# A two-layer decoder trunk on one core: the conditioning product moves from VectorE to four column groups of TensorE, the first projections run by pairs of row blocks, and the convolution's projections become three products of float32r parts

## The chip, the cores and the metric

One Trainium2 chip, one of its cores. The metric is the device time of one execution in microseconds (us), and less is better.

## The reference

256 tokens of width 1024 go through two layers. A vector `c` sets, through `silu(c)` and one large matrix per layer, six vectors of 1024 numbers per layer (shift, scale and gate of the mixer, and of the experts).

```python
cond = silu(c)                                        # 1 x 1024
for layer in range(2):
    mod = cond @ ada_w[layer] + ada_b[layer]          # 1 x 6144
    sh1, sc1, g1, sh2, sc2, g2 = split(mod, 6)
    h = rms_norm(x, norm_mix[layer]) * (1 + sc1) + sh1
    y = nsa_conv_mixer(h) if layer == 0 else rwkv_pool_mixer(h)
    x = x + g1 * y
    h = rms_norm(x, norm_ffn[layer]) * (1 + sc2) + sh2
    x = x + g2 * grouped_moe(h)                       # 16 experts of width 512, 2 per token
return rms_norm(x, final_norm)
```

In layer 0 `h @ w_in` gives queries, keys and values of a sparse attention (compressed blocks, selected blocks, window) and three blocks of 512 columns `xb, bg, cg` of a short convolution, `y = bg * conv3(cg * xb)`. In layer 1 it gives the inputs of an RWKV-7 scan and of a pooling. All data are float32.

## The kernel before, in words

The whole trunk is one program. It has four stages, one after the other: mixer 0 (attention and convolution), the experts of layer 0, mixer 1 (RWKV and pooling), the experts of layer 1. All weights are streamed: SyncE (SP) issues them as tiles of 128 x 2048 float32 (1 MB) into a ring of `NB = 10` buffers named `w`, which grows by some slabs of the mixers when these are free. A load into a ring buffer waits until the buffer's last reader is done, and all loads behind it on SP's queue wait with it.

The order on TensorE (PE) and on SP is written out by hand, as the order in which the Python code emits it. Chains that wait are filled by `Fill`: a list of small units of PE work, each with a cost in us, of which `fill.run(us)` emits as many as make up `us` at the point where it stands. The order on VectorE (DVE), ScalarE (ACT) and GpSimd (POOL) is chosen by a scheduler from a model.

**Conditioning** (`ada`, L203 to L213). `ada_w` is laid out transposed: a tile holds, for 128 output columns on the partitions, the 1024 input weights of two column blocks. `cond` is the vector `silu(c)` on every partition. For each half tile DVE does one pass over 128 x 1024 that multiplies by `cond` and sums along the row (L209), which leaves one column of `modc`; POOL adds the bias (L213). There are 12 groups (`n`) in each layer, of 2 tiles and 4 passes, so 48 MB and 96 passes in all. Layer 0 has all its groups in mixer 0, where layer 1's groups 0 to 2 are done too; group 3 (2 MB) comes between the experts of layer 0 and mixer 1, in `start` (L1618), and the others lie in mixer 1.

**First projections of mixer 0** (L477 to L480, L526 and on). For each half `h` of the rows of the weight: 8 passes of L209 (two groups), 8 transposes of the normed `xn` (L289), the modulation into `hT` (L278 on DVE, L280 on ACT), then the three projections `TokProj` (k and v, q, and the 280 other columns) with four row blocks each.

**Convolution's projections** (`chan_units`, L556). Three groups of 512 columns (xb, cg and bg), each four units of 8 float32 products 128x128 by 128x256 (L566), 96 products in all. They are fill for the waits of the attention.

**Attention**. The hidden part of the compression is `L605` (32-column stationary tiles, so four column groups of the array side by side), the gelu chain ends in `hg` (L625), then L634 and L639 make the compressed keys and values, L653 scores them, `L658` to `L667` are their softmax, L673 transposes it. Ten steps of a pipeline follow: scores L684 and L686, softmax L687 to L699, transposes L709 (evacuated by `evac`, L140 on DVE and L142 on ACT), output L720 and L724, with fill between.

**Experts**. L994 makes gate and up (64-column stationary tiles, two column groups), L1026 down, for 16 experts; the weights of one layer are 96 tiles of 1 MB, a third each for gate, up and down.

**Mixer 1**. Its weights are split into two float32r parts: `split_w` (L396 and L397) casts the high part on ACT and subtracts for the low part on DVE or POOL; `product` (L435) adds hi·hi, hi·lo and lo·hi. The RWKV chunk products L1331, a solve (L1349 and L1354) and its spread follow, then levels (L1383, L1374) and the scan.

Of the kernel before, what the change touches and what calls it, by code (L numbers as in the profile page):

```python
# [22 lines left out]
S = 256  # L23
# [4 lines left out]
NB = 10  # L28
# [68 lines left out]
def trunk(ctx: ExitStack, tc: tile.TileContext, A, out):  # L97
# [49 lines left out]
    nc.scalar.dma_start(cond, bass.AP(tensor=ca.tensor, offset=ca.offset, ap=[[0, 128], [1, D]]))  # L147
    P.activation(cond, cond, AF.Silu)  # L148
    x = act.tile([128, 2, D], F32, name="x")
    for tt in range(2):  # L150
        nc.scalar.dma_start(x[:, tt], A["x"][tt * 128:(tt + 1) * 128, :])
    vec = con.tile([128, NV], F32, name="vec")
# [7 lines left out]
    load_consts(con, "c_all", nc.scalar)  # L160

# [38 lines left out]
    def ada_load(l, n):  # L200
        return [stream(A["ada_w"][l, n, h]) for h in range(2)]

    def ada(l, n, tiles=None, h0=0, cs=(0, 1)):  # L203

        for h, w in enumerate(tiles or ada_load(l, n), h0):
            for c in cs:
                ws = w[:, c * D:(c + 1) * D]
                k = n * 4 + h * 2 + c
                V.scalar_tensor_tensor(ws, ws, 1.0, cond, op0=OP.mult, op1=OP.mult, accum_out=modc[:, l, k:k + 1])  # L209
        if h == 0 or c == 0:  # L210
            return
        o = V_ADAB + l * 48 + n * 4
        G.tensor_tensor(modc[:, l, n * 4:n * 4 + 4], modc[:, l, n * 4:n * 4 + 4], vec[:, o:o + 4], op=OP.add)  # L213

    def ada_pieces(l, n):

        tiles = ada_load(l, n)

        def piece(h, c, after):
            with tc.issue_after(after):  # L220
                ada(l, n, [tiles[h]], h, (c,))

        return [lambda after, h=h, c=c: piece(h, c, after) for h in range(2) for c in range(2)]
# [25 lines left out]
    class Norm:  # L249
# [32 lines left out]
        def scale(self, tt, r):  # L282
            V.tensor_scalar(self.xn[:, tt], x[:, tt], r, None, op0=OP.mult)

# [98 lines left out]
    class WGroup:  # L383


        def __init__(self, src, n):
            self.n = n
            self.h = [stream(src[:, h * 4 * n:(h + 1) * 4 * n], 4 * n) for h in range(2)]

        def __call__(self, kt, lo=0, hi=None):  # L390
            hi = self.n if hi is None else hi
            return self.h[kt // 4][:, (kt % 4) * self.n + lo:(kt % 4) * self.n + hi]
# [45 lines left out]
    def mixer0(after):  # L438
# [23 lines left out]
        class TokProj:  # L462
# [10 lines left out]
            def run(self, h):  # L473
                n = self.n
                for tt in range(2):
                    if h == 0:
                        self.pq[tt] = ps(n)  # L477
                    for k in range(4):
                        kt = h * 4 + k
                        mm(self.pq[tt], hT[:, kt, tt * 128:(tt + 1) * 128], self.w[:, k * n:(k + 1) * n], start=kt == 0, stop=kt == 7)  # L480
                    if h:
# [36 lines left out]
        projs = [TokProj(512, 512, done_k4), TokProj(0, 512, done_q), TokProj(1024, 280, done_k2)]  # L518
        for h in range(2):
            ada(0, h)  # L520
            ada(0, 2 + h)
            norm.ab(h)
            for tt in range(2):
                norm.transposes(tt, h)
            for t in projs:
                t.load(h)  # L526
                if h == 0 and t is projs[0]:
                    load_consts(mp, "c_m0", nc.sync)
                    G.tensor_copy(cbf, K("causal"))
                t.run(h)  # L530
# [3 lines left out]
        for n in (4, 5):  # L534
            ada(0, n)
# [20 lines left out]
        def chan_units(col, done):  # L556
            w = WGroup(W0[:, col * 8:(col + 512) * 8], 512)
            out = []
            for ct in range(4):
                st = {}  # L560

                def unit(q, ct=ct, st=st):
                    if q == 0:
                        st["pq"] = ps(S)
                    for kt in range(q * 4, q * 4 + 4):
                        mm(st["pq"], w(kt, ct * 128, ct * 128 + 128), hT[:, kt, :], start=kt == 0, stop=kt == 7)  # L566
# [3 lines left out]
                out += [(1.73, lambda q=q, u=unit: u(q)) for q in range(2)]  # L570
# [1130 lines left out]
```

## Time and profile before

| what | value |
| --- | --- |
| median of 3 runs | 841.82 us (840.27 to 2588.47) |
| the profiled execution | 841.15 us |
| span of its records | 839.4 us (1.75 us lie around it) |
| mean granted TensorE clock | 0.965 |
| HBM read | 289.4 MB |

The profiled execution is 0.67 us below the median. A row of a timeline reads: start, duration, engine, line and operation, what is written and read, shapes, how many records, and in brackets the idle time of the engine just before with what ended it. A row of groups reads: busy time, mean of one in ns, idle time before them and what ended it. A float32 matmul leaves two records, so "x24" of float32 are 12 products; a product of float32r parts leaves one. The stages are mixer 0 from 0 to 207 us, the experts of layer 0 to 414, mixer 1 to 621, the experts of layer 1 and the end to 839.4.

### The profile page before, as it was taken

What the parts mean: (1) busy time and instruction counts of PE and PEld (TensorE: products, weight loads), DVE (VectorE), ACT (ScalarE), POOL (GpSimd) and SP (SyncE); (2) the same over time, 40 slices, a digit from 0 to 9 for tenths busy, and PEclk for the clock granted to TensorE, in tenths of its full rate; (3) what the DMA queues carried; (4) which work ended last, traced back from release to release, by engine and by line L of the source; (5) the groups of instructions that cost most, each with busy time, mean ns of one, the idle gap of its engine ahead of it and who ended that gap; (6) DMA issues with size and microseconds to landing.
All of it is one profiled execution on the core that took longest, in us unless ns stands there. A gap on an engine that the chain in (4) does not pass through costs nothing. (4 is left out here: it accounts for less than half of the span.)

```text
span 839.4 us, 12129 instructions
## 1 busy us (share of the span) xinstructions
PE 752.2 (90%) x4833; PEld 423.1 (50%) x4834; DVE 440.7 (53%) x937; ACT 222.2 (26%) x442; POOL 101.6 (12%) x87
## 2 busy tenths in 40 slices
PE   0998989897999999999679869999979999999994
PEld 0556766455353353533278859567543534435341
DVE  5566869854122343322788898984531421434225
ACT  3031213244120121111457533303541201202112
POOL 0000132411000000000233793000110000000000
PEclk9999989998999999999879979999989999999998
DMA  9999859797999999999846185885849999999991
GB/s 363 415 421 420 355 195 364 287 419 282 374 422 423 421 422 421 423 420 424 330 189 251 63 324 216 337 317 200 346 177 421 422 422 422 422 422 422 420 417 74
DMA packets 42689, 291.34 MB, mean 347 GB/s; under 512 B 4864, under 2 KB 5504, under 8 KB 8448
## 3 DMA queue, kind: packets, MB, share of 16 engines
q1 hardware_dynamic: 41760, 288.07, 84.6%
q10 hardware_dynamic: 864, 2.40, 0.7%
q8 instruction: 42, 0.69, 0.3%
q14 instruction: 23, 0.19, 0.1%
HBM read 289.40 MB, written 1.05 MB: 346 GB/s over the span
## 5 line engine op out<-in xcount | busy, mean ns | idle before, releaser
L994 PE MATMUL ps<-w,XT 128*64 128x512 f32 x1024 | 223.7, 594 | 0.0
L994 PEld LDWEIGHTS ps<-w,XT 128*64 128x64 f32 x1024 | 75.4, 137 | 144.5 <-issue 140.3
L209 DVE SCALAR_TENSOR_TENSOR w<-w,cond 128x1024 f32<-128x1024 f32 x96 | 118.4, 1263 | 11.4 <-ACT cond L148 6.3
L999 DVE TENSOR_TENSOR sg<-sg,ps 128x512 f32<-128x512 f32 x16 | 11.0, 688 | 199.4 <-PE ps L994 199.4
L1026 PE MATMUL ps<-w,HT 128*64 128x512 f32 x512 | 113.8, 596 | 1.3 <-ACT HT L1013 1.3
L1026 PEld LDWEIGHTS ps<-w,HT 128*64 128x64 f32 x512 | 35.2, 137 | 70.5 <-issue 63.0
L435 PE MATMUL ps<-hT,wr 128*128 128x256 f32 x288 | 56.0, 297 | 5.6 <-issue 4.1
L370 PE MATMUL ps<-w,slab 128*128 128x512 f32 x128 | 59.7, 604 | 0.0
L1031 DVE SCALAR_TENSOR_TENSOR Y<-ps,gw,Y 128x512 fp32r<-128x512 f32 x32 | 24.0, 751 | 62.8 <-ACT Y L1030 62.8
L397 POOL TENSOR_TENSOR wr<-w,wr 128x2048 fp32r<-128x2048 f32 x5 | 24.7, 4945 | 224.1 <-SPq L1088 211.6
L435 PEld LDWEIGHTS ps<-hT,wr 128*128 128x128 f32 x288 | 47.6, 203 | 6.6 <-issue 4.6
L1030 ACT ACTIVATE Y<-ps,gw 128x512 fp32r<-128x512 f32 x32 | 21.9, 686 | 98.2 <-PE ps L1026 98.2
L381 DVE TENSOR_TENSOR x<-x,ps 128x512 f32<-128x512 f32 x72 | 46.3, 681 | 0.3
L566 PE MATMUL ps<-hT,w 128*128 128x256 f32 x192 | 46.1, 397 | 0.0
L380 DVE TENSOR_TENSOR ps<-ps,gb 128x512 f32<-128x512 f32 x64 | 41.4, 693 | 2.6 <-PE ps L1046 2.4
L435 PE MATMUL ps<-lo,wr 128*128 128x256 f32 x144 | 42.3, 294 | 0.0
L1046 PE MATMUL ps<-Y,CT 128*128 128x512 f32 x128 | 39.0, 421 | 2.9 <-ACT Y L1030 1.7
L566 PEld LDWEIGHTS ps<-hT,w 128*128 128x128 f32 x192 | 37.3, 199 | 6.1 <-issue 0.8
L480 PE MATMUL ps<-w,hT 128*128 128x512 f32 (+1 forms) x96 | 36.8, 544 | 0.3 <-ACT hT L280 0.2
L998 ACT ACTIVATE sg<-ps 128x512 f32<-128x512 f32 x16 | 9.6, 597 | 98.6 <-PE ps L994 98.6
L280 ACT ACTIVATE XT<-ps,AB 128x256 f32<-128x256 f32 x32 | 18.0, 563 | 62.2 <-PE ps L909 50.8
L370 PEld LDWEIGHTS ps<-w,slab 128*128 128x128 f32 x128 | 22.8, 190 | 22.4 <-issue 21.3
(321 smaller groups left out, 959.9 us busy)
## 6 DMA issues: line engine op xcount, KB each, us to landing
w<-in_moe_g_dram SPq DMA_DIRECT2D x64, 1024.0 KB, 16.0
w<-in_moe_u_dram SPq DMA_DIRECT2D x64, 1024.0 KB, 15.0
w<-in_moe_d_dram SPq DMA_DIRECT2D x60, 1024.0 KB, 16.1
w<-in_ada_w_dram SPq DMA_DIRECT2D x48, 1024.0 KB, 9.4
w<-in_w_dram SPq DMA_DIRECT2D x19, 1024.0 KB, 11.6
w<-in_wout_dram SPq DMA_DIRECT2D x8, 1024.0 KB, 9.7
w<-in_cmp_w_dram SPq DMA_DIRECT2D x4, 1024.0 KB, 12.6
w<-in_moe_d_dram SPq DMA_DIRECT2D x4, 512.0 KB, 17.9
```

Of the source, the lines that this page charges most:

```text
L209: V.scalar_tensor_tensor(ws, ws, 1.0, cond, op0=OP.mult, op1=OP.mult, accum_out=modc[:, l, k:k + 1])
L370: mm(st[h], self.oT(kt)[:, tt * 128:(tt + 1) * 128], self.ws[h][kt // 4][:, (kt % 4) * 512:(kt % 4 + 1) * 512], start=kt == 4, stop=kt == 3)
L380: V.tensor_mul(po, po, gb[:, sl])
L381: V.tensor_add(x[:, tt, sl], x[:, tt, sl], po)
L397: eng.tensor_tensor(lo, raw, hi, op=OP.subtract)
L435: mm(pq, a, b, start=first and kt == kts[0] and i == 0, stop=last and kt == kts[-1] and i == 2)
L480: mm(self.pq[tt], hT[:, kt, tt * 128:(tt + 1) * 128], self.w[:, k * n:(k + 1) * n], start=kt == 0, stop=kt == 7)
L566: mm(st["pq"], w(kt, ct * 128, ct * 128 + 128), hT[:, kt, :], start=kt == 0, stop=kt == 7)
L994: mm(pg[64 * e:64 * e + 64, :], XT[:, kt, 64 * e:64 * e + 64], ws[kt // 4, e][:, (kt % 4) * 512:(kt % 4 + 1) * 512], start=kt == 0, stop=k ...
L1026: mm(py[64 * e:64 * e + 64, :], HT[:, c, 64 * e:64 * e + 64], ws[e][:, c * 512:(c + 1) * 512], start=c == 0, stop=c == 3)
L1031: V.scalar_tensor_tensor(Y[:, 1, sl], py, gw, Y[:, 0, sl], op0=OP.mult, op1=OP.subtract)
L1046: mm(po, CT[:, tt], Y[:, i, h * 512:(h + 1) * 512], start=i == 0, stop=i == 1)
```

## The change

1. Of the conditioning only layer 0's groups 0 to 3 (16 passes, `cols`) stay on DVE. The other 40 tiles (same bytes, another layout, `ada_q`) are multiplied on PE by units of four matmuls, one for each column group, with a column of `silu(c)` spread to 32 columns as the stationary tile (L234 of the changed kernel). Eight units add up to one bank; ACT copies it (L238), four small matmuls (L243) turn it into columns, and DVE adds the bias (L246). The units are fill: 24 in mixer 0, 16 in mixer 1. Layer 1's group 3 is done in mixer 0 with the others of its 16 columns, so `start` has no conditioning left.
2. At the start `c` comes through two queues, and all loads of ACT's queue are issued before its first activation. The first projections run by pairs of row blocks: 4 passes, 4 transposes and two modulations, then k/v and q of that pair; the 280 other columns once per half.
3. The convolution's weights and `hT` are split into float32r parts, and each of the 96 products becomes three. The parts take ring buffers, two for each raw tile.
4. The ring has 11 buffers, and the gate's transposes, the load of the output projection and the pace of the fill have moved.

```diff
-NB = 10
+NB = 11
...
-    nc.scalar.dma_start(cond, bass.AP(tensor=ca.tensor, offset=ca.offset, ap=[[0, 128], [1, D]]))
-    P.activation(cond, cond, AF.Silu)
+    for eng, o in ((nc.sync, 0), (nc.scalar, 64)):
+        eng.dma_start(cond[o:o + 64], bass.AP(tensor=ca.tensor, offset=ca.offset, ap=[[0, 64], [1, D]]))
...
     load_consts(con, "c_all", nc.scalar)
+    P.activation(cond, cond, AF.Silu)
+    P.activation(ccol, ccol, AF.Silu)
...
-    def ada(l, n, tiles=None, h0=0, cs=(0, 1)):
-        for h, w in enumerate(tiles or ada_load(l, n), h0):
-            for c in cs:
-                ws = w[:, c * D:(c + 1) * D]
-                k = n * 4 + h * 2 + c
-                V.scalar_tensor_tensor(ws, ws, 1.0, cond, op0=OP.mult, op1=OP.mult, accum_out=modc[:, l, k:k + 1])
...
+        def unit(self, l, g, kt, w):
+            if kt == 0:
+                self.bank = ps(512)
+            for q in range(4):
+                mm(self.bank[32 * q:32 * q + 32, :], ccol[:, kt:kt + 1].to_broadcast([128, 32]), w[:, q * 512:(q + 1) * 512],
+                   start=kt == 0, stop=kt == 7)
+            if kt == 7:
+                self.row = con.tile([128, 512], F32, name="arow", tag="arow")
+                P.copy(self.row, self.bank)
+
+        def columns(self, l, g):
+            pc = ps(4, 4)
+            for c in range(4):
+                mm(pc[:, c], self.row[:, c * 128:(c + 1) * 128], ident[:, ::32], start=True, stop=True)
+            o = V_ADAB + l * 48 + g * 16
+            f = lambda t: t.rearrange("p (q c) -> p c q", q=4)
+            V.tensor_tensor(f(modc[:, l, g * 16:g * 16 + 16]), pc, f(vec[:, o:o + 16]), op=OP.add)
...
+        nxt = norm.pair(0)
         for h in range(2):
-            ada(0, h)
-            ada(0, 2 + h)
...
+            for q in (2 * h, 2 * h + 1):
+                for n in (h, 2 + h):
+                    cols(n, q % 2, 1 if q else 2)
+                norm.mod_pair(q, nxt)
+                for t in projs[:2]:
+                    if q % 2 == 0:
+                        t.load(h)
+                    t.run(q)
+                    if t is projs[0] and q < 3:
+                        nxt = norm.pair(q + 1)
+            projs[2].load(h)
...
+        for h in range(2):
+            sl = slice(4 * h, 4 * h + 4)
+            P.copy(hi[h], hT[:, sl])
+            V.tensor_tensor(lo[:, sl], hT[:, sl], hi[h], op=OP.subtract)
...
-            w = WGroup(W0[:, col * 8:(col + 512) * 8], 512)
+            w = WGroup(W0[:, col * 8:(col + 512) * 8], 512).split()
...
-                        mm(st["pq"], w(kt, ct * 128, ct * 128 + 128), hT[:, kt, :], start=kt == 0, stop=kt == 7)
+                        wh, wl = w(kt, ct * 128)
+                        for i, (a, b) in enumerate(((wh, hi[q][:, kt % 4]), (wh, lo[:, kt]), (wl, hi[q][:, kt % 4]))):
+                            mm(st["pq"], a, b, start=kt + i == 0, stop=kt == 7 and i == 2)
```

On PE, between the making of the compressed keys (L639) and the transposes of their softmax (L673), the program of before has:

```order
18 L639 MATMUL ps<-w_108,hg 32x64 x8
19 L566 MATMUL ps<-hT,w 128x256 x4
20 L653 MATMUL ps<-kcT,slab_98 128x16 x16
21 L566 MATMUL ps<-hT,w 128x256 x8
22 L673 MATMUL ps<-c_all,slab_102 128x128 x4
```

At the same place the changed program has the rows below (L712 is L639, L726 is L653, L637 the convolution's products, L234 the conditioning's); the `wr` that L637 reads after L726 are the parts of the second convolution group:

```order
93 L712 MATMUL ps<-w_112,hg 32x64 x8
94 L234 MATMUL ps<-w,ccol 32x512 x16
95 L726 MATMUL ps<-kcT,slab_102 128x16 x16
96 L637 MATMUL ps<-hi,wr 128x256
97 L637 MATMUL ps<-lo,wr 128x256
98 L637 MATMUL ps<-hi,wr 128x256 x2
```

Four conditioning units now stand ahead of the scores, and the products behind them read parts that ACT and DVE make, where before they read the tile as it had landed.

On ACT, at the same place of the changed program, L734 is the exponential of the compressed softmax and L441 the cast of a convolution weight to its high part (before had L661 and no cast there):

```order
41 L651 COPY slab_103<-ps 128x256 x2
42 L734 ACT_TABLE_LOAD
43 L734 ACTIVATE s_653<-s_653 128x128
44 L734 ACTIVATE s_675<-s_675 128x128
45 L441 CAST wr<-w 128x2048 x2
46 L142 COPY PcT<-ps 128x256
47 L764 ACTIVATE slab_105,mx<-ps,mx 128x128 x4
48 L441 CAST wr<-w 128x2048 x2
```

The casts of the second group stand behind the two exponentials, which read the result of the scores.

On PE, between two late steps of the attention's pipeline, the changed program has (L793 and L797 are the output of a step, before's L720 and L724; L782, L757 and L759 are transposes and scores, before's L709, L684 and L686):

```order
279 L243 MATMUL ps<-c_all,arow 128x4 x4
280 L234 MATMUL ps<-w,ccol 32x512 x20
281 L782 MATMUL ps<-c_all,slab_105 128x128 x4
282 L757 MATMUL ps<-slab_106 128x512 x2
283 L759 LDWEIGHTS ibf
284 L759 MATMUL ps<-cbf,ibf 128x2x128
285 L759 LDWEIGHTS ibf
286 L759 MATMUL ps<-cbf,ibf 128x2x128
287 L793 MATMUL ps<-slab_104,slab_108 64x128 x2
```

Five units stand between the output of one step and the transposes of the next, where before had convolution products; between the transposes and the output there is no fill in either.

## Rows read from the trace of the kernel before

**Rows 1.** Page, part 1: busy time, share of the span, instructions of each engine.

```profile
PE 752.2 (90%) x4833; PEld 423.1 (50%) x4834; DVE 440.7 (53%) x937; ACT 222.2 (26%) x442; POOL 101.6 (12%) x87
```

**Rows 2.** Windows by stage: length, busy time by engine, granted clock, DMA share, GB/s.

```profile
0.00:207.00 207.00, 166.23 (x886) 109.64 (x887) 141.19 (x365) 59.15 (x156) 33.15 (x43) 0.97 0.90 357
207.00:414.00 207.00, 204.02 (x1013) 86.08 (x1012) 66.20 (x117) 36.18 (x58) 0.79 (x1) 1.00 0.99 410
414.00:621.00 207.00, 176.84 (x1925) 141.19 (x1925) 162.82 (x333) 90.58 (x167) 67.69 (x44) 0.91 0.63 244
```

**Rows 3.** Page, part 5: the group of the conditioning passes.

```profile
L209 DVE SCALAR_TENSOR_TENSOR w<-w,cond 128x1024 f32<-128x1024 f32 x96 | 118.4, 1263 | 11.4 <-ACT cond L148 6.3
```

**Rows 4.** Timeline of PE in the experts of layer 0: one pair of tiles.

```profile
230.69 13.90 PE L994 MATMUL ps<-w,XT 128*64 128x512 f32 x64
```

**Rows 5.** Timeline of PE: products in four column groups.

```profile
67.53 1.93 PE L605 MATMUL ps<-w,slab 128*32 128x256 f32 x32 [1.90 <-DVE slab L548]
```

**Rows 6.** Timeline of PE in mixer 1: forms that follow each other.

```profile
524.96 1.13 PE L1295 MATMUL ps<-slab,c_m 128*128 128x256 f32 x4
525.93 0.38 PE L190 MATMUL ps<-zb 128*128 128x512 bf16 x1
526.24 1.15 PE L1383 MATMUL ps<-c_m,slab 64*64 64x64 f32 x32
```

**Rows 7.** Timeline of PE in mixer 1: products of float32r parts.

```profile
475.07 0.28 PE L435 MATMUL ps<-lo,wr 128*128 128x256 f32 x1
475.19 0.40 PE L435 MATMUL ps<-hT,wr 128*128 128x256 f32 x2
475.42 0.28 PE L435 MATMUL ps<-lo,wr 128*128 128x256 f32 x1
```

**Rows 8.** Timeline of PE in mixer 0: two units of the convolution, and two later.

```profile
98.54 5.35 PE L566 MATMUL ps<-hT,w 128*128 128x256 f32 x24
...
108.02 0.47 PE L720 MATMUL ps<-slab,slab 128*64 128x128 f32 x1 [2.38 <-DVE slab L140]
...
109.69 7.74 PE L566 MATMUL ps<-hT,w 128*128 128x256 f32 x24
```

**Rows 9.** Timeline of PE around the compressed softmax.

```profile
80.99 0.42 PE L634 MATMUL ps<-hg,w 128*64 128x16 f32 x8 [1.15 <-DVE hg L625]
...
83.64 1.96 PE L653 MATMUL ps<-kcT,slab 64*128 64x16 f32 x32
...
90.98 0.63 PE L673 MATMUL ps<-c_all,slab 128*128 128x128 f32 x4 [1.73 <-DVE slab L667]
```

**Rows 10.** Timeline of ACT there: the second exponential.

```profile
86.94 0.31 ACT L661 ACTIVATE s<-s 128x128 f32<-128x128 f32 x1 [0.21 <-DVE s L660]
```

**Rows 11.** Durations (least, median, most, in ns) of the casts of split_w.

```profile
L396 ACT CAST wr<-w x9: 1882/1909/1936, 411.2 to 472.1; 128x2048 fp32r<-128x2048 f32 x9
```

**Rows 12.** The same of its subtractions on DVE.

```profile
L397 DVE TENSOR_TENSOR wr<-w,wr x4: 2292/3540/5317, 437.6 to 477.9; 128x2048 fp32r<-128x2048 f32 x4
```

**Rows 13.** Groups on PE in mixer 0: steps of the attention's pipeline.

```profile
L709 PE MATMUL ps<-c_all,slab 128*128 128x128 f32 x48 | 6.8, 275 | 1.8 <-POOL slab L699 1.8
L720 PE MATMUL ps<-slab,slab 128*64 128x128 f32 x48 | 6.3, 299 | 5.4 <-DVE slab L140 4.6 <-ACT slab L142 0.8
```

**Rows 14.** Timeline of PE at the start.

```profile
21.03 1.94 PE L289 MATMUL ps<-c_all,xn 128*128 128x128 f32 x8 [21.03 <-DMA c_all<-in_c_all_dram]
23.14 1.22 PE L480 MATMUL ps<-w,hT 128*128 128x512 f32 x1 [0.18 <-ACT hT L280]
```

**Rows 15.** Timeline of ACT at the start: the second half of x has landed.

```profile
15.23 0.63 ACT L236 ACTIVATE junk<-x 128x512 bf16<-128x512 f32 x1 [2.34 <-DMA x<-in_x_dram]
```

**Rows 16.** Timeline of PE at the start of mixer 1.

```profile
421.40 3.65 PE L289 MATMUL ps<-c_all,w 128*128 128x128 f32 x16 [8.26 <-DVEq L1088]
429.11 0.77 PE L435 MATMUL ps<-hT,wr 128*128 128x256 f32 x2 [4.06 <-issue]
```

**Rows 17.** Timeline of DVE there: the last conditioning pass ahead of the modulation.

```profile
421.46 5.18 DVE L209 SCALAR_TENSOR_TENSOR w<-w,cond 128x1024 f32<-128x1024 f32 x1 [0.26 <-DVEq L1088]
```

**Rows 18.** Timeline of PE in mixer 1: the solve.

```profile
498.28 3.71 PE L1354 MATMUL ps<-c_m,slab 64*64 64x16 f32 x64 [6.09 <-DVE slab L1335]
```

**Rows 19.** Timeline of PE in mixer 1: the pooling's second product.

```profile
533.32 0.67 PE L1449 MATMUL ps<-pool,pw 128*128 128x256 f32 x2 [1.17 <-DVE pool L1447]
```

More of the change, by code (lines that the diff above doesn't have):

```diff
@@ L215, in ada_pieces, with __init__, load, last @@
[L215 to L223, printed above, removed]
+    class Ada:
+        def __init__(self):
+            self.todo = deque((l, g, kt) for l, g in ((0, 1), (0, 2), (1, 0), (1, 1), (1, 2)) for kt in range(8))
+            self.bank, self.end = None, None
+        def load(self, n):
+            out = []
+            for _ in range(n):
+                l, g, kt = self.todo.popleft()
+                if kt == 0 and self.end:
+                    out.append((0.6, self.end))
+                    self.end = None
+                w = stream(A["ada_q"][l, g, kt])
+                out.append((0.9, lambda l=l, g=g, kt=kt, w=w: self.unit(l, g, kt, w)))
+                if kt == 7:
+                    self.end = lambda l=l, g=g: self.columns(l, g)
+            return out
+        def last(self):
+            e, self.end = self.end, None
+            return [(0.6, e)]
+        def unit(self, l, g, kt, w):
[4 more added lines that the diff above has]
+                   start=kt == 0, stop=kt == 7)
+            if kt == 7:
+                self.row = con.tile([128, 512], F32, name="arow", tag="arow")
[7 more added lines that the diff above has]
+            V.tensor_tensor(f(modc[:, l, g * 16:g * 16 + 16]), pc, f(vec[:, o:o + 16]), op=OP.add)
@@ L736, in mixer0 @@
                 st_out(*tr.popleft())
+            if i == 2:
+                fill.add(gate_units(0, 2, gb))
+            if i == 2:
+                op.load(1, 0)
             if i == 6:
-                fill.all()
                 fill.add(op.units(0))
-            fill.run(5 if i < 6 else 2)
+            fill.run(5 if i < 6 else 3)
             if more[i]:
-                ada(*more[i])
+                fill.add(aq.load(more[i]))
+            if i == 4:
+                fill.add(aq.last())
             if i:
@@ L1083, in moe @@
         s_scatter(7, 1)
-        last = next_norm()
+        next_norm()
         mctx.close()
@@ L1523, in mixer1 @@
         gb = buf["vR"]
-        todo = deque()
-        for _ in range(3):
-            todo.extend(ada_pieces(1, rest.popleft()))
+        fill.add(aq.load(4))
         st = {}
@@ L1534, in step @@
             if steps == 0 and spent >= 2:
-                last = solve()
-                for _ in range(4):
-                    todo.popleft()(last)
+                solve()
                 steps = 1
@@ L1541, in step @@
                 steps = 2
-        for _ in range(4):
-            todo.popleft()(ins)
         step(0)
@@ L1606, in mixer1 @@
         head_norm(3)
-        ada(1, rest.popleft())
+        fill.add(aq.last())
         fill.run(1)
@@ L1617, in trunk, with start @@
     state, fin = [], []
-    def start(pool, l, rms, xs, todo, last):
+    def start(pool, l, rms, xs):
         norm = Norm(l, 0, rms, xs, pool)
         preload(AF.Sigmoid, xs[:, 1, 0:1])
-        norm.ab(0)
-        for tt in range(2):
-            d = norm.transposes(tt, 0)
-        for h, t in enumerate(todo):
-            with tc.issue_after(d[1] if h else last):
-                ada(1, 3, [t], h)
-        norm.ab(1)
-        for tt in range(2):
-            d = norm.transposes(tt, 1)
+        for h in range(2):
+            norm.ab(h)
+            for tt in range(2):
+                d = norm.transposes(tt, h)
         return norm, d
```

128 lines of the change are left out of this document (71 added, 57 removed).

## Prediction

> **What bounds the kernel now.** I read the busy shares first. TensorE (PE) is busy for 752.2 us of 839.4, VectorE (DVE) for 440.7 [rows 1]. A cut through the stages comes next, because such a share is a mean [rows 2]. In the experts of layer 0 PE is busy for 204.02 of 207 us at clock 1.00 while the DMA share is 0.99. PE is the bound there, its tiles follow each other at 13.90 us a pair [rows 4], and the change touches nothing in it. Mixer 0 has 166.23 us of PE work in 207, mixer 1 has 176.84 at a mean clock of 0.91. What lies beside this is idle time of PE: 41 us in the first (21 before its first matmul [rows 14]) and 30 in the second.
>
> The change takes 80 of 96 passes from DVE, 80 x 1.26 = 101 us [rows 3]. DVE is not the bound, so these microseconds are worth only what PE waits for them; and the same product becomes work of the engine that is the bound. This sets the sign: PE's added work against the idle time that goes.
>
> **Mixer 0, term by term**, in us, plus is slower.
>
> *Units, +20.9.* A unit is four matmuls of 512 float32 columns, one in each column group. Sixteen matmuls of 256 columns in four groups took 1.93 [rows 5], 0.241 for 512 columns, so 0.96 for a unit with the start and end of the burst in it. A pair of tiles in the experts is 32 matmuls of 512 columns in two groups in 13.90, which makes 0.87 for a round of two [rows 4]. If four groups run as fully side by side as two, a unit is one round, 0.87. I take that, since units mostly come in bursts; bounds 0.87 and 0.96. 24 units make 20.9 (up to 23.0).
>
> *Changes of the array's form, +1.3.* L190 starts 0.16 before the end of the matmul ahead of it, which has the same form (524.96 + 1.13 against 525.93); L1383, of another form, only 0.07 before the end of L190 (525.93 + 0.38 against 526.24) [rows 6]. So a change of form costs some 0.09, twice for each of 7 bursts. The Trainium skill, "TensorEngine Tiling (Array Packing)", section "Tiling Modes", says that changing the tiling mode, not just the tile, drains the TensorE, which speaks against units strewn one by one; the rows agree in kind, and with no such cost the total would be 3 less.
>
> *Columns, +1.3.* Three times four small matmuls. The nearest row is L634, 4 products in 0.42 [rows 9]; bounds 0 and 1 each.
>
> *Convolution, -7.3.* Before: 24 records, that is 12 products, in 5.35, so 0.44 with the end, 0.43 without; 96 make 41 [rows 8]. After: 288 products of float32r parts. Three of these take 475.42 - 475.07 = 0.35, or 0.117 each [rows 7], together 33.7.
>
> *A new wait at the second group of the convolution, +6.6.* Before, the compressed scores L653 end at 85.60 [rows 9] and convolution products follow, which wait for nothing. After, the products there read parts. On ACT their casts stand behind the two exponentials, of which the second ended at 87.25 [rows 10], 1.65 after the scores; then 1.91 for each cast [rows 11] and 2.29 for each subtraction on DVE, if POOL leaves it alone [rows 12]. PE's first part comes 3.6 after the scores, the low part at 5.85, and the second tile's low part at about 8.2, with 1.6 of products in between: 6.6 idle. What is queued behind these products is the whole attention pipeline. Bounds: 0, if ACT reaches the casts early, and 9, if the subtraction takes 3.5 as its median did.
>
> *Waits that go, -11.2.* L605 loses 1.90 [rows 5]: its input waited on a DVE full of passes. L634 loses 1.15 and L673 1.73 [rows 9]. L720 waited 5.4 in all and L709 1.8 [rows 13]; units and a lighter DVE should take L720's away and half of L709's, 6.4. If the splits on DVE take the place of the passes, 3 of this comes back.
>
> *Half clock, 0.* Two units took 7.74 instead of 5.35 behind an idle time of 2.38 at L720 [rows 8]. The new wait of 6.6 would cause the like, so this moves rather than goes; bounds -2.4 and +2.4.
>
> *Start, -4.0.* The first product came at 23.14 behind eight transposes that waited for `c_all` until 21.03 [rows 14]. `c_all` is now issued before ACT's first activation. What is late next is `x`: its second half was there at 15.23 [rows 15], and its squares, root, scaling, four transposes and a modulation take some 4 more, which gives 19.1. Bounds -2 (`x` shares the DMA engines with more) and -6.
>
> *Smaller ones, +2.2.* The low part of `hT` stands on DVE ahead of the passes of the last pair: half of 2.29 [rows 12], 1.2. The last conditioning tiles and the output projection wait in SP's queue for ring buffers that hold parts; a tile at 410 GB/s [rows 2] is 2.6 us, and I take 1 (0 to 5).
>
> Sum for mixer 0: 20.9 + 1.3 + 1.3 - 7.3 + 6.6 - 11.2 - 4.0 + 2.2 = +9.8.
>
> **Experts, 0.** PE-bound; they need tiles ahead because DMA runs at 0.99, and the ring has one more buffer. If mixer 0 leaves fewer tiles ahead, PE waits at the end of the stage: up to +5.
>
> **Mixer 1.** Units 16 x 0.87 = +13.9, changes of form 9 x 0.18 = +1.6, columns +0.8. Two units stand ahead of chunk products that wait for POOL, so they are hidden: -1.7. At its start L435 came at 429.11, 7.7 after the transposes began [rows 16], because a DVE pass took 5.18 beside POOL [rows 17] and the modulation stood behind it; without it, -3.6 (bounds 0, if POOL stretches something else, and -5). The pooling's wait of 1.17 [rows 19] goes, -1.2. Ahead of the solve PE idles 6.09 for DVE [rows 18]; I take -2.5 of it. Sum +7.3.
>
> **Total.** 841.15 + 9.8 + 7.3 = 858.25, so 858. It is made against the profiled execution, 0.67 below the median of 841.82, which I let stand.
>
> **Rivals.**
>
> *PE's waits on the other engines go for good.* Place: the products behind the compressed scores. If the casts are done before PE arrives, the new wait (-6.6) and the drop of the clock (-2.4) go, and with DVE this light the late tiles and the low part (-2.2), 2 more at the start and the rest of the 6.09 (-3.6) too: 858.3 - 16.8 = 841, not slower than before. For it: 5.4 of L720's waits and the 6.09 have DVE as releaser. Against it: the casts stand behind the exponentials in ACT's order. It decides if that wait is under 2 us.
>
> *The ring and the splits cost more.* Parts hold ring buffers, DVE's subtraction at 3.54 rather than 2.29, late tiles (+4 beyond my 1), 3 of the attention's waits back, the experts short of tiles (+3), and the wait at 9 (+2.4): 871. For it: DMA is at 0.99 when the experts run, so a tile that comes late there isn't made up. Against it: in mixer 1 the DMA share is 0.63.
>
> *Four column groups don't run side by side as two do.* At 0.96 a unit, 40 units make 3.6 more; if only three of four ran side by side, 1.16 a unit, 11.6 more: 870. Against it: sixteen products of 256 columns in 1.93 are 3.55 times as fast as 0.43 each [rows 5, 8]. The Trainium skill, "TensorE: Matmul & The Clock Gate", section "Part 3: Packing small matmuls", gives 2.38 times for three column tiles; at that ratio a unit would be an estimated 1.1. The row of this kernel stands against it.
>
> *More than that goes.* To be faster by 2%, 17 us, PE would have to lose 17 + 35 + 5 - 7, about 50 us, of the 71 that it idles in the mixers, of which some 19 at the start and 8 ahead of mixer 1's transposes hang on loads and norms.
>
> **How the numbers follow.** My forecast (852 to 865) gets 0.48, the first rival 0.18, the second 0.20, the third 0.08, a gain of over 2% 0.06. What a measurement of this kernel can tell from no change is about 2%, 825 to 858.7. My forecast lies at that edge and gives half to each side; with the first rival the middle gets 0.24 + 0.18 + a little of the others, 0.46; slower gets 0.24 + 0.20 + 0.08 less that little, 0.48; faster 0.06. The range takes in the first rival and some of what lies beyond it, and the second: 837 to 874.
>
> **What would show it.** L234 at 0.87 a unit; the experts of layer 0 starting near 217 and running 207 us; a PE wait of 5 to 9 us for `wr` behind L726; no wait for DVE at L605's successor; first product at 18 to 21; L435 of mixer 1 some 4 us after its transposes begin. It is wrong if units lie in waits that PE has anyway, if L726's products start at once, or if the experts' stage grows.

## The result, and the profile after

The changed kernel takes 863.85 us (median of 4 runs, 863.6 to 865.38) against 841.86 us before: a ratio of 1.028 on record, 95% interval 1.0263 to 1.0296 (the two medians alone give 1.026), so slower by nearly 3%. The forecast was 858, with a range from 837 to 874. The profiled execution took 864.05 us, its span 862.0 us, 22.6 more than before. The differences below are between the two profiled executions. One of the four runs of the kernel before took 2588.47 us, the others 840.27 to 841.89.

Part 1 of the page answers to [rows 1], the windows by stage to [rows 2]. The stages have moved, so the windows are cut at the changed kernel's own borders: its gate and up product L1071 first runs at 221.90 and, in layer 1, at 642.85.

```profile
PE 787.1 (91%) x5289; PEld 434.2 (50%) x5290; DVE 366.3 (42%) x798; ACT 236.6 (27%) x452; POOL 76.0 (9%) x63
```

```profile
0.00:221.90 221.90, 182.72 (x1196) 115.73 (x1197) 109.89 (x298) 72.33 (x164) 19.38 (x28) 0.96 0.88 350
221.90:428.50 206.60, 204.42 (x1013) 85.42 (x1012) 65.24 (x115) 36.12 (x57) 0.00 (x0) 1.00 0.96 397
428.50:642.85 214.35, 194.33 (x2069) 147.48 (x2069) 120.82 (x264) 91.92 (x169) 56.64 (x35) 0.91 0.61 237
```

DVE lost 74 us, from 440.7 to 366.3, and POOL 26. PE gained 35, from 752.2 to 787.1. Mixer 0 is 14.9 us longer: 16.5 more of PE work (182.72 against 166.23), and idle time of 39.2 against 40.8, hardly less. The experts' window is as long as it was. To measure mixer 1, the first transposes of its start are the better border: they begin at 435.58, against 421.40 in [rows 16]. From the start of the experts of layer 0 to there it is 213.7 us (214.4 before), from there to the experts of layer 1 207.3 (199.9), and from there to the end 219.2 (218.1). So 14.9 - 0.7 + 7.4 + 1.0 = 22.6, and mixer 0 and mixer 1 are where the loss lies.

The units of the conditioning on PE's timeline, a burst of four in mixer 0:

```profile
81.27 3.64 PE L234 MATMUL ps<-w,ccol 128*32 128x512 f32 x32
```

and later, in mixer 1's scan, a single unit:

```profile
573.78 1.06 PE L234 MATMUL ps<-w,ccol 128*32 128x512 f32 x8
```

Four units take 3.64 and one 1.06: 0.86 for each and 0.20 for the burst, and four column groups of 512 columns do run as fully side by side as two [rows 4].

Behind the compressed scores (L726, before's L653) PE waits for the parts of the second convolution group, as the order of ACT had said. Where [rows 9] have one idle time of 1.73, PE's timeline now has two, 3.48 and 1.53, and then products at half speed until 96.6:

```profile
84.84 1.96 PE L726 MATMUL ps<-kcT,slab 64*128 64x16 f32 x32
90.28 0.58 PE L637 MATMUL ps<-hi,wr 128*128 128x256 f32 x1 [3.48 <-ACT wr L441]
...
92.61 0.80 PE L637 MATMUL ps<-hi,wr 128*128 128x256 f32 x2 [1.53 <-DVE wr L442]
...
95.98 0.63 PE L637 MATMUL ps<-hi,wr 128*128 128x256 f32 x2
...
96.62 0.43 PE L637 MATMUL ps<-hi,wr 128*128 128x256 f32 x2
...
97.36 0.40 PE L637 MATMUL ps<-hi,wr 128*128 128x256 f32 x2
...
97.71 0.40 PE L637 MATMUL ps<-hi,wr 128*128 128x256 f32 x2
...
98.55 0.60 PE L746 MATMUL ps<-c_all,slab 128*128 128x128 f32 x4
```

Three products (two with `hi`, one with `lo`) step by 0.64 from 95.98 and by 0.35 from 97.36: the granted clock in the window from 80 to 100 is 0.83 (below), which is the lower of two levels for a part of it. The transposes behind all this (L746) come 7.6 us later than L673 did.

Half speed is in the kernel before too, only later: there the window from 100 to 120 has the 0.83 (below).

Later in mixer 0 units wait for their own tiles. PE's timeline has three such waits, 3.6 us in all, and a fourth for the copy of the row on ACT:

```profile
143.78 1.06 PE L243 MATMUL ps<-c_all,arow 128*128 128x4 f32 x8 [0.70 <-ACT arow L238]
...
154.07 1.07 PE L234 MATMUL ps<-w,ccol 128*32 128x512 f32 x8 [1.42 <-DMA w<-in_ada_q_dram]
...
161.56 1.07 PE L234 MATMUL ps<-w,ccol 128*32 128x512 f32 x8 [0.77 <-DMA w<-in_ada_q_dram]
164.05 1.06 PE L234 MATMUL ps<-w,ccol 128*32 128x512 f32 x8 [1.43 <-DMA w<-in_ada_q_dram]
```

The columns L243 take 1.06 each. What DMA does meanwhile is to be seen in windows (length, busy time by engine, granted clock, DMA share, GB/s), of the changed kernel:

```profile
80.00:100.00 20.00, 14.99 (x142) 11.41 (x141) 10.18 (x26) 6.23 (x7) 0.00 (x0) 0.83 0.72 276
100.00:120.00 20.00, 19.17 (x162) 14.80 (x162) 14.97 (x37) 9.12 (x29) 3.60 (x6) 1.00 0.54 218
140.00:160.00 20.00, 17.79 (x157) 8.39 (x160) 8.55 (x25) 7.28 (x25) 3.79 (x4) 1.00 1.01 419
160.00:180.00 20.00, 17.10 (x106) 8.81 (x99) 3.42 (x12) 3.39 (x11) 1.91 (x2) 1.00 1.01 419
```

and of the kernel before:

```profile
100.00:120.00 20.00, 17.62 (x88) 13.14 (x87) 13.40 (x37) 3.55 (x18) 4.47 (x5) 0.83 0.66 238
```

DMA is busy for only 0.72 and 0.54 between 80 and 120 (1.01 and 0.66 before, so a part of this rest is old), where the loads stand behind ring buffers, and is full from 140 to 180, where the units wait. The waits of SP's queue from 20 to 200 us (in total, times, longest) name the holders of the buffers:

```profile
SPq L134 <- PE ps L637: 36.0, 3, 15.1
SPq L134 <- PE ps L234: 25.3, 20, 4.0
...
SPq L134 <- DVE wr L442: 17.6, 4, 7.2
```

L637 are the products that read the parts, L442 is the subtraction that makes them. The list alone doesn't show that the parts are to blame: with float32 products in their place (second experiment) SP waits 44.4 for those, against 36.0 and 17.6 here.

At the start ([rows 14, 15]), PE's and ACT's timelines:

```profile
20.81 5.76 PE L526 MATMUL ps<-w,hT 128*128 128x512 f32 x8 [0.66 <-ACT hT L305]
...
50.13 10.91 PE L526 MATMUL ps<-w,hT 128*128 128x512 f32 x32 [1.30 <-ACT hT L305]
60.97 1.15 PE L612 MATMUL ps<-c_all,slab 128*64 128x64 f32 x32
```

with, in the kernel before, as the first row behind the projections:

```profile
60.82 1.16 PE L543 MATMUL ps<-c_all,slab 128*64 128x64 f32 x32
```

```profile
12.81 0.21 ACT L164 ACTIVATE ccol<-ccol 128x8 f32<-128x8 f32 x1 [3.54 <-DMA ccol<-in_c_t_dram]
12.93 0.61 ACT L261 ACTIVATE junk<-x 128x512 bf16<-128x512 f32 x1
```

The first product comes at 20.81, 2.3 earlier than before. But the projections end at 60.97, and before they ended at 60.82. ACT stood 3.54 us for `ccol`, the 4 KB column of `c`, and the squares of `x` stood behind it. The wait of 1.30 ahead of the last pair has another cause. DVE's timeline:

```profile
45.43 1.23 DVE L601 TENSOR_TENSOR lo<-hT,hi 128x1024 fp32r<-128x1024 f32 x1 [3.80 <-PE ps L315]
```

This is the low part of `hT`. It takes the buffer of `xn`, so DVE stood 3.80 us in front of it until the last transposes (L315) were done, and the passes of the last pair stood behind it. In the second experiment, which makes no parts, they ran 4.8 us earlier.

In mixer 1 the places of [rows 16, 18] read:

```profile
435.58 3.67 PE L330 MATMUL ps<-c_all,w 128*128 128x128 f32 x16 [7.14 <-ACTq L1163]
440.67 0.77 PE L480 MATMUL ps<-hT,wr 128*128 128x256 f32 x2 [1.42 <-POOL wr L442]
```

```profile
498.25 0.80 PE L480 MATMUL ps<-hT,wr 128*128 128x256 f32 x2 [4.42 <-ACT slab L1413]
...
507.10 3.70 PE L1429 MATMUL ps<-c_m,slab 64*64 64x16 f32 x64 [2.99 <-DVE slab L1410]
```

L480 now follows 5.1 us after the transposes began, not 7.7, and the solve's idle time is 2.99, not 6.09; a wait of 4.42 ahead of L480 is where 1.51 was. The stage is 7.4 longer all the same.

### The profile page after: what moved, and what is told of

Read it like the earlier page. It is cut to its first block, busy times and chain, and to the rows that moved or that the text cites. A ratio compares the mean times of both kernels' runs of the same rounds, so it can differ in the third digit from the quotient of the medians.

```text
span 862.0 us, 12905 instructions
## 1 busy us (share of the span) xinstructions
PE 787.1 (91%) x5289; PEld 434.2 (50%) x5290; DVE 366.3 (42%) x798; ACT 236.6 (27%) x452; POOL 76.0 (9%) x63
## 4 chain that ended last, share of the span: by engine, by line
PE 40%; DVE 5%; ACT 3%; issue 2%; POOL 1%; POOLq 0%; DVEq 0%; ACTq 0%
PE ps L1071 13%; PE ps L1103 6%; PE ps L1458 4%; PE ps L480 4%; PE ps L411 3%; PE ps L1123 2%; PE ps L986 1%; PE ps L234 1%; PE ps L194 1%; DVE slab L1365 1%; DVE slab L1410 0%; POOL wr L442 0%; DVE ps L421 0%; PE ps L1429 0%; ACT wr L441 0%
## 5 line engine op out<-in xcount | busy, mean ns | idle before, releaser
L1071 PE MATMUL ps<-w,XT 128*64 128x512 f32 x1024 | 223.1, 593 | 0.0
L1071 PEld LDWEIGHTS ps<-w,XT 128*64 128x64 f32 x1024 | 73.6, 137 | 145.7 <-issue 143.4
L480 PE MATMUL ps<-hT,wr 128*128 128x256 f32 x288 | 57.6, 302 | 5.8 <-ACT slab L1413 4.4
L480 PEld LDWEIGHTS ps<-hT,wr 128*128 128x128 f32 x288 | 48.9, 208 | 7.6 <-ACT slab L1413 4.7
L480 PE MATMUL ps<-lo,wr 128*128 128x256 f32 x144 | 43.0, 299 | 0.0
L442 POOL TENSOR_TENSOR wr<-w,wr 128x2048 fp32r<-128x2048 f32 x5 | 22.9, 4589 | 223.4 <-PE ps L1123 212.3
L637 PE MATMUL ps<-hi,wr 128*128 128x256 f32 x192 | 38.0, 295 | 5.0 <-ACT wr L441 3.5
L234 PE MATMUL ps<-w,ccol 128*32 128x512 f32 x320 | 38.3, 598 | 3.7 <-DMA w<-in_ada_q_dram 3.6
L637 PEld LDWEIGHTS ps<-hi,wr 128*128 128x128 f32 x192 | 31.5, 198 | 5.8 <-ACT wr L441 3.6
```

Of the source, the lines that this page charges most:

```text
L234: mm(self.bank[32 * q:32 * q + 32, :], ccol[:, kt:kt + 1].to_broadcast([128, 32]), w[:, q * 512:(q + 1) * 512], start=kt == 0, stop=kt == 7)
L480: mm(pq, a, b, start=first and kt == kts[0] and i == 0, stop=last and kt == kts[-1] and i == 2)
L637: mm(st["pq"], a, b, start=kt + i == 0, stop=kt == 7 and i == 2)
L1071: mm(pg[64 * e:64 * e + 64, :], XT[:, kt, 64 * e:64 * e + 64], ws[kt // 4, e][:, (kt % 4) * 512:(kt % 4 + 1) * 512], start=kt == 0, stop=k ...
```

## The experiments

At first the theory was that of the forecast: a unit is time of TensorE, and nothing hides it. The rival: the loss is in waits around the units. All numbers with a ratio were measured beside runs of the kernel before on the same chip.

**Thin units.** 

```diff
-                mm(self.bank[32 * q:32 * q + 32, :], ccol[:, kt:kt + 1].to_broadcast([128, 32]), w[:, q * 512:(q + 1) * 512],
+                mm(self.bank[32 * q:32 * q + 32, 0:32], ccol[:, kt:kt + 1].to_broadcast([128, 32]), w[:, q * 512:q * 512 + 32],
...
-                P.copy(self.row, self.bank)
+                P.copy(self.row.rearrange("p (a b) -> p a b", b=32), self.bank[:, None, 0:32].to_broadcast([128, 16, 32]))
```

> The changed kernel with every conditioning unit multiplying 32 columns instead of 512, so most of the conditioning is left out; its tiles, its four column groups, its changes of form and its waits stay. Theory (the units are TensorE time that nothing hides): a unit falls from about 0.95 us to 0.2, 40 units give back 26 to 31 us, 833 to 838. Rival (the loss is in the waits around the units: late tiles, casts, changes of form): under 12 us come back, over 852.

Measured: 853.8 us, ratio to before 1.0145 (1.0103 to 1.0186). Some 11 us came back by the ratios, the rival's number. By stage: mixer 1 took 199.2 us from its transposes on, 8.1 less than with whole units. Mixer 0 took 223.1, which is 1.2 more; but the profiled execution, at 856.14, is the slowest of the four (849.99 to 856.14), so that the stage gets longer is shown for this one alone. PE's timeline there:

```profile
138.12 1.15 PE L243 MATMUL ps<-c_all,arow 128*128 128x4 f32 x8 [3.67 <-ACT arow L238]
...
149.08 0.30 PE L234 MATMUL ps<-w,ccol 128*32 128x32 f32 x8 [3.33 <-DMA w<-in_ada_q_dram]
151.57 0.34 PE L234 MATMUL ps<-w,ccol 128*32 128x32 f32 x8 [2.19 <-DMA w<-in_ada_q_dram]
...
159.06 0.27 PE L234 MATMUL ps<-w,ccol 128*32 128x32 f32 x8 [1.16 <-DMA w<-in_ada_q_dram]
161.55 0.27 PE L234 MATMUL ps<-w,ccol 128*32 128x32 f32 x8 [2.22 <-DMA w<-in_ada_q_dram]
```

```profile
140.00:160.00 20.00, 12.65 (x116) 7.65 (x114) 5.78 (x14) 6.06 (x21) 1.96 (x3) 0.77 1.02 421
160.00:180.00 20.00, 17.81 (x87) 10.75 (x88) 3.42 (x12) 2.10 (x6) 1.91 (x2) 0.74 1.01 420
```

The tiles arrive when they arrive: the last unit ran at 164.05 with whole units and runs at 161.55 with thin ones. What PE doesn't do it waits (3.33, 2.19, 1.16, 2.22 and 3.67 for a copy). In these windows, with 12.65 and 17.81 us of work in 20, its granted clock is 0.77 and 0.74, where with whole units it was 1.00, and the products behind run slower; by the router's transposes the 2.5 us are lost. In all, the units' records shrank by 18.8 us in mixer 0 and PE's idle time there grew by 9.3 (48.5 against 39.2); its other records grew by 10.6. In mixer 0 the theory falls, in mixer 1 it holds.

**The convolution in float32 again.**

```diff
-        for h in range(2):
-            sl = slice(4 * h, 4 * h + 4)
-            P.copy(hi[h], hT[:, sl])
-            V.tensor_tensor(lo[:, sl], hT[:, sl], hi[h], op=OP.subtract)
...
-            w = WGroup(W0[:, col * 8:(col + 512) * 8], 512).split()
+            w = WGroup(W0[:, col * 8:(col + 512) * 8], 512)
...
-                        wh, wl = w(kt, ct * 128)
-                        for i, (a, b) in enumerate(((wh, hi[q][:, kt % 4]), (wh, lo[:, kt]), (wl, hi[q][:, kt % 4]))):
-                            mm(st["pq"], a, b, start=kt + i == 0, stop=kt == 7 and i == 2)
+                        mm(st["pq"], w.raw[kt // 4][:, (kt % 4) * 512 + ct * 128:(kt % 4) * 512 + ct * 128 + 128], hT[:, kt, :],
+                           start=kt == 0, stop=kt == 7)
```

> The changed kernel with the convolution's 96 products in float32 again, no splits. Theory (TensorE time rules): the products cost 7 us more, the wait for parts behind the compressed scores (5.0) and the half clock after it (some 2) go, so 862 to 866. Rival (the parts' ring buffers and the splits hold everything up, the late conditioning tiles too): 853 to 859.

Measured: 858.19 us, ratio 1.0213 (1.0182 to 1.0244), against 1.028 with the parts, the rival's number. So the three products with all that makes their parts, on which the forecast counted for -7.3 beside a new wait of 6.6, cost some 5.7 (the two intervals leave 2 to 10). Mixer 0 is 7.1 shorter without them in the profiled execution, which at 855.29 is the quickest of its four, 2.9 below the median. PE's windows show it without the two waits, at full clock:

```profile
80.00:100.00 20.00, 20.00 (x157) 15.10 (x157) 9.81 (x38) 4.15 (x13) 1.31 (x2) 1.00 0.84 338
100.00:120.00 20.00, 20.00 (x131) 13.09 (x130) 8.91 (x28) 4.92 (x23) 2.54 (x4) 1.00 0.79 316
```

and its timeline the last pairs of the projections and the last unit:

```profile
44.65 14.24 PE L526 MATMUL ps<-w,hT 128*128 128x512 f32 x40
...
156.91 1.06 PE L234 MATMUL ps<-w,ccol 128*32 128x512 f32 x8 [0.22 <-DMA w<-in_ada_q_dram]
```

PE has 20.00 of 20 from 80 to 120. DMA rests less, with shares of 0.84 and 0.79, and of the four waits of units and columns two are left, 0.71 and 0.22. The wait of 1.30 ahead of the last pair is gone, and the projections end at 58.82, 2.0 before those of the kernel before. This divides the 7.1: PE's idle time in mixer 0 falls by 11.0 (28.2 against 39.2: 5.0 behind the scores, 3.4 for tiles, 1.3 in the projections and smaller ones), and PE's work grows by 3.8, since the float32 products take 43.0 where the parts' products took 38.3.

**The first projections by halves.** The loop of before, in the changed kernel:

```diff
-            for q in (2 * h, 2 * h + 1):
-                for n in (h, 2 + h):
-                    cols(n, q % 2, 1 if q else 2)
-                norm.mod_pair(q, nxt)
...
+            for n in (h, 2 + h):
+                cols(n, 0)
+                cols(n, 1)
+            norm.ab(h)
+            for tt in range(2):
+                norm.transposes(tt, h)
...
```

> The changed kernel with the first projections by halves of the rows again (8 passes, 8 transposes, then three projections), all else as changed. Theory (the pairs bring the first product forward by 2.3 us and lose it again before the projections end, at 60.97 against 60.82 before): 863 to 866. Rival (the pairs keep their 2.3 us and more, because the passes of a half come late): 867 to 872.

Measured: 873.71 us, ratio 1.039 (1.0351 to 1.0428), against 1.028 with the pairs: over 9 us slower, the rival, and more. The first product came at 28.45. ACT's timeline:

```profile
16.51 0.21 ACT L164 ACTIVATE ccol<-ccol 128x8 f32<-128x8 f32 x1 [8.14 <-DMA ccol<-in_c_t_dram]
```

Here ACT waited 8.14 us for `ccol`. The squares of `x` stood behind it, and DVE stood 5.45 us for the sum of these with five of the eight passes behind. So this doesn't price the pairs alone: the column's later landing is in it.

**The column later.** Its activation stands behind the projections in the code. ACT's order is the scheduler's, though, and it placed the activation in front of the squares of the second half of `x`, with a table load before and behind it (below).

```diff
-    P.activation(ccol, ccol, AF.Silu)
...
+        P.activation(ccol, ccol, AF.Silu)
         nc.sync.dma_start(w2, A["cmp_w2"])
```

> The changed kernel with the activation of the small column ccol issued after the first projections and not ahead of the squares of x. Theory (ScalarE stands 3.54 us waiting for the 4 KB of ccol, with the squares of x behind it, and this eats the start's gain): first product 2 to 3.5 us earlier and the end as much, 860 to 862. Rival (the pairs' tiles and passes bound the projections, whatever the first product does): the first product moves and the end doesn't, 863 to 864.

Measured: 863.15 us, ratio 1.0266 (1.0234 to 1.0297), which can't be told from the changed kernel's 1.028. ACT's timeline (L601 is now the activation of `ccol`):

```profile
11.85 1.28 ACT L601 ACT_TABLE_LOAD   x1
13.14 0.21 ACT L601 ACTIVATE ccol<-ccol 128x8 f32<-128x8 f32 x1
13.37 1.28 ACT L265 ACT_TABLE_LOAD   x1
```

So ACT no longer waits 3.54 for the column, but spends 2.8 on it with the two table loads. The first product came at 19.96, 0.85 earlier, the projections ended at 59.66, 1.3 earlier, and mixer 0 1.5 earlier. The total lies where the rival had it, but its reason isn't borne out: the end moved with the first product. It is the theory at a smaller size, and what the start gains with the column out of the way altogether isn't measured in this kernel.

**The units behind the scores.** The four units run while ACT and DVE make the parts.

```diff
         fill.add(aq.load(2))
-        fill.run(3)
...
         fill.add(aq.load(2))
-        fill.run(3)
+        fill.run(6.5)
```

> The changed kernel with the four conditioning units ahead of the compressed scores moved behind them, where TensorE waits 3.48 and 1.53 us for parts. Theory (the wait is for casts that stand behind the exponentials, and 3.6 us of units fit into it): 3 to 5 us less, 859 to 861. Rival (the wait is set by the second raw tile, whose load waits for ring buffers that the units and the parts hold, so it comes later by as much): 0 to 1 less, 863 to 864.

Measured: 859.35 us, ratio 1.0213 (1.0173 to 1.0253), 4.5 less by the medians. PE's timeline has one wait of 1.81 where there were two of 5.0:

```profile
88.49 0.58 PE L637 MATMUL ps<-hi,wr 128*128 128x256 f32 x2 [1.81 <-DVE wr L442]
```

Mixer 0 ends 4.4 earlier. So the wait is for the casts and the subtractions, and units that wait for neither fill it. The waits of later units for tiles stay as they were, 3.6 in all.

**Thin units and no parts.** The edits of the first two experiments together. Now there were two theories on mixer 0: held buffers, or the stream of tiles itself.

> The thin units (32 of 512 columns, most of the conditioning left out) together with the convolution in float32, so no parts hold ring buffers. Theory A (with parts, mixer 0 waits for tiles behind held ring buffers, and thin units only wait longer; without parts TensorE is the bound and the units are its time): mixer 0 gets 14 to 18 us shorter than with float32 convolution alone and mixer 1 some 9, so 830 to 836. Theory B (the stream of tiles itself bounds mixer 0, parts or not): mixer 0 gets under 6 us shorter, 843 to 849.

Measured: 842.64 us, ratio 1.0019 (1.0002 to 1.0035). Mixer 0 got 6.4 shorter than with the float32 convolution alone (208.3 against 214.8), mixer 1 10.0 (197.1 against 207.1). That is much nearer to theory B. Without parts PE waits again where whole units had kept it busy, 7.7 in all for their tiles; the last unit:

```profile
150.09 0.27 PE L234 MATMUL ps<-w,ccol 128*32 128x32 f32 x8 [2.49 <-DMA w<-in_ada_q_dram]
```

```profile
120.00:140.00 20.00, 15.42 (x196) 9.46 (x194) 10.88 (x34) 8.90 (x32) 5.66 (x6) 0.91 1.00 403
140.00:160.00 20.00, 15.52 (x126) 10.07 (x120) 5.40 (x16) 4.54 (x13) 1.91 (x2) 0.83 1.02 422
160.00:180.00 20.00, 18.86 (x77) 10.10 (x76) 4.17 (x10) 5.18 (x9) 0.00 (x0) 1.00 1.01 419
```

DMA is full from 120 to 180. A thin burst of four takes 0.53 where a whole one took 3.64, so 24 units gave up 18.5 us of PE, and mixer 0 got 6.4 of it back. The other 12.1 went two ways: PE's idle time grew by 7.5 (35.7 against 28.2), nearly all of it for tiles, and its other records by 4.6, at a granted clock of 0.91 and 0.83 where there had been 1.00. So 7.5 of the units' time had lain beside the stream of tiles, and the rest was lost to the clock. From the last unit's start to the end of mixer 0 it is 57.9 us in the changed kernel, 57.9 without parts and 58.3 here: in these three the end of mixer 0 moved with the last unit (in the first experiment, at the lower clock, it is 61.6).

The three ratios divide the loss: 1.028 with everything, 1.0213 without the parts, 1.0019 without parts and with thin units. That makes 0.7% for the convolution's parts, 1.9% (some 16 us) for the columns that the units multiply, and 0.2% for all else, its savings with its costs. With the parts in place the same columns came to 11 us (the first experiment), so the shares depend on the order.

**What helps, put into the kernel before.** Group 3 of layer 1 goes to mixer 0, on DVE as all others.

```diff
-        more = [(0, 9), (0, 10), (0, 11), None, None, None, None, (1, 0), (1, 1), (1, 2)]
+        more = [(0, 9), (0, 10), (0, 11), (1, 3), None, None, None, (1, 0), (1, 1), (1, 2)]
...
-        for h, t in enumerate(todo):
-            with tc.issue_after(d[1] if h else last):
-                ada(1, 3, [t], h)
...
```

> The kernel before with layer 1's conditioning group 3 done on VectorE in mixer 0, behind the third attention step, and not between the experts and mixer 1, where a pass took 5.18 us ahead of the modulation. Theory (this is the part of the change that helps, and it needs no TensorE): 3 to 5 us less than before, 836 to 838.5. Rival (2 MB and 5 us of VectorE more in mixer 0 cost as much as they save): 840 to 843.

Measured: 837.48 us, ratio 0.9959 (0.9944 to 0.9974), 0.4% faster than the kernel before, which is little, but its interval doesn't reach 1. Mixer 0 is 2.5 longer (the experts start at 209.48), mixer 1 5.1 shorter (194.7 from the transposes on). PE's timeline, for [rows 16]:

```profile
423.66 3.47 PE L289 MATMUL ps<-c_all,w 128*128 128x128 f32 x16 [6.90 <-DVEq L1086]
428.97 0.47 PE L435 MATMUL ps<-hT,wr 128*128 128x256 f32 x2 [1.85 <-POOL wr L397]
```

L435 now follows 5.3 us after the transposes began, at full clock (0.47 for its first records, against 0.77). That is 2.4 of the 5.1.

**The same with the changed start**, without `ccol`.

```diff
...
-            ada(0, h)
-            ada(0, 2 + h)
-            norm.ab(h)
...
+            for q in (2 * h, 2 * h + 1):
+                for n in (h, 2 + h):
+                    cols(n, q % 2, 1 if q else 2)
+                norm.mod_pair(q, nxt)
...
```

> The kernel of e7_before_13 with the changed start as well (c through two queues, c_all ahead of the first activation, projections by pairs), without ccol and without any unit. Theory (the pairs save time where nothing waits for ccol; by halves the changed kernel took 9.8 us more): another 3 to 6 us less, 831 to 835. Rival (in the kernel before the projections are bound by tiles that DMA brings at 419 GB/s): 836 to 839, no more than e7_before_13.

Measured: 837.8 us, ratio 0.9953 (0.993 to 0.9975), no more than without it. The first product came at 18.88 and the projections ended at 57.35, 3.5 earlier, but the hidden part of the compression then waited for DVE, and ran at the lower clock:

```profile
65.61 3.19 PE L641 MATMUL ps<-w,slab 128*32 128x256 f32 x32 [3.45 <-DVE slab L584]
```

1.93 had sufficed for it [rows 5]. Mixer 0 ended at 209.84, against 209.48 without the new start: here the earlier start only moved the wait.

**The same with a buffer more**, and the changed kernel's size of the DMA scratch, which makes room for it.

```diff
-NB = 10
+NB = 11
...
-    nc = _bacc.Bacc("TRN2", target_bir_lowering=False, num_devices=1)
+    nc = _bacc.Bacc("TRN2", target_bir_lowering=False, num_devices=1, dynamic_dma_scratch_size=64)
```

> The kernel of e7_before_13 with 11 ring buffers in place of 10. Theory (mixer 0's tiles come late because loads wait for ring buffers, so one more lets the 2 MB in earlier): the 2.5 us that mixer 0 got longer in e7_before_13 come back in part, 834.5 to 836.5. Rival (DMA is full where the tiles are late, a buffer more changes nothing): 837 to 838.

Measured: 837.16 us, ratio 0.996 (0.9942 to 0.9978): the rival. One buffer more changes nothing that can be measured here.

## Why the prediction was right, and where its terms were off

The direction and its reason stood: with 101 us of DVE passes only some waits of PE went, 10.5 us in mixer 0 and some 9 in mixer 1, and the product came back as work of the engine that is the bound. PE gained 35 us and the kernel 22.6, where the sum had said 17.1. In mixer 0, 14.9 against the forecast's 9.8, the trace shows where the difference is. The terms of work (20.9 + 1.3 + 1.3 - 7.3) make 16.2, and PE's work grew by 16.5; that it fits so well is in part luck, since the columns took 1.9 more than said and the outputs of the pipeline 2.0 less (9.6 against 11.6), which no term had. The terms of waiting (6.6 - 11.2 - 4.0 + 2.2) make -6.4, and PE's idle time fell by 1.6: the start and the late tiles were mis-sized. By its own steps:

- *Units, +20.9 in mixer 0 and +13.9 in mixer 1, with changes of form +1.3 and +1.6.* In records 22.7 and 15.6, so the price was right, 0.86 a unit and 0.20 a burst. That nothing hides them was wrong in mixer 0: without them only 6.4 of 18.5 came back, 7.5 turned into waits for tiles and the rest into a lower clock. In mixer 1 most of it was paid (8.1 and 10.0 of some 12.5).
- *Columns, +1.3 and +0.8.* 1.06 each, 3.2 and 2.1. L634, which wrote 64 partitions, was too far a row for products of 128 by 128.
- *Convolution, -7.3.* The products are as cheap as said (0.35 for three at full clock; 38.3 in all, against 46.1), but the whole edit costs about 5.7. Its costs stood in the sum as terms of their own: the wait behind the scores at +6.6 (it was 5.0), the low part of `hT` at +1.2 (1.30) and the late tiles at +1 (3.6, of which 3.4 go without the parts). With them the edit came to +1.5 in the forecast. What was mis-sized is the late tiles. And of the -7.3, which fits 46.1 and 38.3, only 4.7 is left where the float32 products run at full clock, as in the second experiment (43.0). The half clock at 0, as a drop that moves, was right: before it fell between 100 and 120, after between 80 and 100.
- *Waits that go, -11.2.* L605's, L634's, L673's, L709's and 3.9 of the 5.4 of L720's did go, 10.5 in all. In their place came 5.0 for parts, 3.6 for tiles (forecast 1), 0.70 for a copy of the row, 1.30 in the projections (forecast 1.2) and some smaller ones, so the idle time of mixer 0 fell by only 1.6.
- *Start, -4.0.* -2.3 at the first product and nothing where it counted: the projections ended 0.15 later than before. Two things were missed or kept apart from it: `ccol` (3.54 on ACT), and the low part of `hT` with its 1.30. Without the parts the projections ended at 58.82, so the pairs do keep 2.0 where no part stands in their way.
- *Mixer 1, +7.3.* +7.4 was measured. The start's -3.6 was -2.6, the solve's -2.5 was -3.1, the pooling's wait went; the wait of 4.42 ahead of L480 was not foreseen.
- *Experts, 0.* -0.7 in layer 0; in layer 1, with the end of the kernel, +1.0.

Of the rivals, the first (waits go for good) had its point of decision at 2 us of wait behind the scores; it was 5.0, and it fell. The second was right on the tiles alone: 3.6 for them, of the 5 that it had; the wait behind the scores was under 6.6 and not 9, the attention's waits stayed away and the experts weren't short. The total lay between it and the forecast. The third fell: 0.86 a unit. With it falls the estimate of 1.1 that was made with the ratio for three column tiles in the Trainium skill, "TensorE: Matmul & The Clock Gate", section "Part 3: Packing small matmuls". That a change of tiling mode drains TensorE (the Trainium skill, "TensorEngine Tiling (Array Packing)", section "Tiling Modes") isn't contradicted by the 0.20 that each burst costs on top; but this holds the burst's own start and end too, and no run takes them apart.

What stays open: why the tiles come late with the parts. The units behind the scores bring 4.4 in mixer 0 and leave the waits for tiles as they were; the float32 convolution brings 7.1 and takes these waits away. That the buffers held by the parts are the reason is argued from SP's queue and DMA's rest, not shown: nothing was run with parts that hold no buffer. And no run moves the conditioning alone, without the other three changes.

## What to carry to other kernels

Work taken from an engine that isn't the bound is worth the waits it caused and no more, so count those waits first, and then ask for each what stands in the queue behind it: here the small gain (a stretched pass ahead of mixer 1) could be had by moving one group of loads, without the new product. A product that is cheaper by the record can cost more by its operands, when other engines must make them first: here 5.0 us of wait at one place, and later tiles. And where the stream of weights is near its limit, a part of PE's work is free, and what is removed can come back as waits and as a lower clock: thin the work out once, and see.

## What was not expected of the hardware

The 4 KB of `ccol` were issued at 2.74 us, on ACT's queue behind the two loads of `x`, and had not landed before 12.8: 10.1 us, where the 512 KB loads of `x` took 8.9. A small transfer wasn't fast here among large ones. And taking work from PE slowed it: with thin units its granted clock from 160 to 180 was 0.74 and not 1.00, and in the profiled execution, the slowest of the four, mixer 0 ended 1.2 us later than with sixteen times the columns.
